# First weights over a second DMA queue, gamma scaled on POOL, a column for variance plus epsilon

## The chip, the cores and the metric

The kernel runs on one core of a Trainium2 chip. The core has five engines that work from queues of their own: PE (matrix multiply), DVE (vector), ACT (activation functions), POOL (general purpose) and SP (here it only starts transfers). The metric is the device time of one execution in microseconds, taken as the median over runs. In the profile, "PEld" is the loading of weights into PE, which overlaps its matmuls, and "SPq", "ACTq", "POOLq" stand for instructions that an engine's sequencer handles, such as the start of a DMA transfer.

## The reference

One layer of a decoder over 512 tokens of width 1024 in float32. Cut to what matters:

```python
proj = h @ w_in                                   # q, k, v, pool input, gates
y_attn = moba_attention(q, k, v, rel_bias) @ w_branch_attn
y_pool = multiscale_pool(p, w_pool_group, pool_scale) @ w_branch_pool
mixed  = sigmoid(g0) * y_attn + sigmoid(g1) * y_pool
h = layer_norm(ALPHA * h + mixed @ w_out, ln1_g, ln1_b)
a, u = split(h @ w_ffn_in)
f = (gelu(causal_dwconv(a, conv_w, conv_b)) * u) @ w_ffn_out
h = layer_norm(ALPHA * h + f, ln2_g, ln2_b)

def layer_norm(x, g, b):
    mu = x.mean(-1); var = ((x - mu) ** 2).mean(-1)
    return (x - mu) * rsqrt(var + 1e-5) * g + b
```

## The kernel before

Every matrix product is made of three passes: each float32 operand is split into a rounded high part (`hi`, type fp32r) and a remainder (`lo`), and `mm3` (lines 144 to 148) adds hi x hi, hi x lo and lo x hi into one PSUM bank. The splitting is done by `split` (line 63): ACT copies the source into `hi` (line 67) and DVE subtracts `hi` from the source (line 68). A caller may pass another function for the copy; for the first tile of x that is DVE's `tensor_copy`.

Weights come in chunks of 128 x 1024 elements. `fetch` (line 92) takes the next chunk of a fixed list, starts its transfer from SP (line 108) into one of three raw buffers (tag `wraw`), and splits it into one of five `whi` and `wlo` buffers. `weights(i)` calls `fetch` until it is three chunks ahead of the matmuls. The very first chunk is fetched in two halves of 512 columns, and between the two the second half of the first x tile is loaded (the `early` argument). `load_x` (line 171) loads and splits the eight tiles of the transposed x. Before all of this PE makes eight matmuls on zeros (`WARM`, line 168), and ACT runs an activation on one column (line 164), which loads its function table.

The stages in order: the value projection (line 240); the other input projections interleaved with the attention heads; the two branch projections and their merge (`mt`, line 437, on POOL, then split into `mx_hi` and `mx_lo`); the output projection (`wo`); the first normalization; the feed-forward input (`fi`) with convolution and gelu; the feed-forward output as seven products of a block scheme (`PRODUCTS`, line 40); the second normalization and the stores. The program text gives each engine's order only in part: a scheduler places instructions of independent work on each engine by a time model, so work written later can stand ahead of work written earlier. On one engine everything then runs in its queue's order, so an instruction that waits holds back what stands behind it.

In the seven products the left operands alternate between two buffers, `sd[0]` and `sd[1]`, and the splits of the next product's operand (`sd_hi`, `sd_lo`) are placed as soon as the columns that they overwrite have been read. The weights of some products are formed in the buffer `tw`: after `tw` has been split, a transfer started from POOL adds the next weights to it (line 134).

The two normalizations share their code. `ln_rows` (line 447) loads one gamma row and one beta row, spread over all 128 partitions, by a transfer started from POOL, and multiplies the gamma by -0.5 on ACT (line 450). In the second normalization it is called behind the sixth product, and SP then copies the beta rows to the output (line 711), onto which finished rows are added later. `moments` (line 470) aggregates mean and variance on DVE, takes the root of variance plus epsilon on ACT (`rstd` column 0) and adds epsilon to the variance on DVE (line 474). `centre` (line 484) computes (x - mu) times the scaled gamma, `invert` (line 477) takes the reciprocal of the root and improves it by one step with variance plus epsilon, and `rescale` (line 488) multiplies by the result and adds beta. The last 128 rows go through `finish` (line 508), where DVE's order is the written one.

Of the kernel before, what the change touches and what calls it, by code (L numbers as in the profile page):

```python
# [8 lines left out]
F32 = mybir.dt.float32  # L9
F32R = mybir.dt.float32r  # L10
AF = mybir.ActivationFunctionType
ALU = mybir.AluOpType
PSUM = bass.MemoryType.PSUM

P = 128
# [3 lines left out]
NT = S // P  # L19
# [8 lines left out]
EPS = 1e-5  # L28
# [3 lines left out]
LEAD = 3  # L32
RING = 5
TMP = 4
WARM = 8
NKEEP = 12
NLATE = 4
KH = NF // 2
# [5 lines left out]
def layer_kernel(ctx: ExitStack, tc: tile.TileContext, xT, x, w_v, w_c, rel_bias, invcnt, w_group,  # L44
                 pscale, w_br, w_out, lnr, w_fi, convp, w_fo, out):
    nc = tc.nc
    const = ctx.enter_context(tc.tile_pool(name="const", bufs=1))
# [8 lines left out]
    def bank(name):  # L56
        return ps.tile([P, S], F32, tag="ps", name=name)
# [5 lines left out]
    def split(hi, lo, src, copy=None):  # L63
        if copy:
            copy(hi, src)
        else:
            nc.scalar.activation(hi, src, AF.Copy)  # L67
        nc.vector.tensor_tensor(lo, src, hi.bitcast(F32), op=ALU.subtract)  # L68
# [9 lines left out]
    chunks = [w_v[c] for c in range(4)]  # L78
# [13 lines left out]
    def fetch(pool=None, early=None):  # L92
        i = state["next"]
        state["next"] = i + 1
        if isinstance(chunks[i], tuple):
            ready[i] = fetch_fo(i, *chunks[i])
            return
        raw = wp.tile([P, D], F32, tag="wraw", name=f"wraw{i}", bufs=3)
        if pool is None:
            hi = wp.tile([P, D], F32R, tag="whi", name=f"whi{i}", bufs=RING)  # L100
            lo = wp.tile([P, D], F32R, tag="wlo", name=f"wlo{i}", bufs=RING)
        else:
            hi = pool.tile([P, D], F32R, name=f"whi{i}")
            lo = pool.tile([P, D], F32R, name=f"wlo{i}")
        parts = 2 if early else 1
        for c in range(parts):
            sl = slice(c * (D // parts), (c + 1) * (D // parts))
            nc.sync.dma_start(raw[:, sl], chunks[i][:, sl])
            split(hi[:, sl], lo[:, sl], raw[:, sl])
            if c == 0 and early:  # L110
                early()
        ready[i] = (hi, lo)
# [7 lines left out]
    def fetch_fo(i, name, c):  # L120
        sl = piece(c)
        n = sl.stop - sl.start
        step = {"T3": "=B11", "B11": "+B12", "T1": "+B22", "T2": "+B21", "T4": None}
        if name in step:
            raw = tw[:, sl]
        else:
            raw = wp.tile([P, D], F32, tag="wraw", name=f"wraw{i}", bufs=3)[:, :n]
            nc.sync.dma_start(raw, half(name, sl))
        hi = wp.tile([P, D], F32R, tag="whi", name=f"whi{i}", bufs=RING)[:, :n]
        lo = wp.tile([P, D], F32R, tag="wlo", name=f"wlo{i}", bufs=RING)[:, :n]  # L130
        split(hi, lo, raw)
        then = step.get(name)
        if then and then[0] == "+":
            nc.gpsimd.dma_start(raw, half(then[1:], sl), accum_op=ALU.add)  # L134
        elif then:
            nc.sync.dma_start(raw, half(then[1:], sl))
        return hi, lo

    def weights(i):
        while state["next"] <= min(i + LEAD, state["limit"]):  # L140
            fetch()
        return ready[i]
# [6 lines left out]

    def split3(v, a):  # L150
        return tuple(t.rearrange("p (a c) -> p a c", a=a) for t in v)

    xT_hi = act.tile([P, KT, S], F32R, tag="actT_hi", name="xT_hi")
    xT_lo = act.tile([P, KT, S], F32R, tag="actT_lo", name="xT_lo")
# [12 lines left out]
    wb_ = bank("warm_ps")  # L167
    for i in range(WARM):
        nc.tensor.matmul(wb_, warm[:, :P], warm, start=True, stop=True)
# [5 lines left out]
    for kt in range(KT):  # L175
        xr = aw.tile([P, S], F32, tag="tmp", name=f"xr{kt}", bufs=TMP)
        if kt == 0:
            load_x(kt, xr, slice(0, 256), nc.vector.tensor_copy)
            fetch(early=lambda: load_x(kt, xr, slice(256, 512), nc.vector.tensor_copy))
        else:  # L180
            load_x(kt, xr)
            if kt % 2 == 0:
                fetch()
# [44 lines left out]
    for kt in range(KT):  # L228
        wh, wl = split3(weights(kt // 2), 2)
        wh, wl = wh[:, kt % 2, :], wl[:, kt % 2, :]  # L230
        xs_ = [(xT_hi[:, kt, j * P:(j + 1) * P], xT_lo[:, kt, j * P:(j + 1) * P]) for j in range(NT)]
        last = kt == KT - 1
        if last:
            for j in range(NT):
                mm3(bs[j], xs_[j], (wh, wl), False, True)
                nc.scalar.activation(vv[:, j, :], bs[j], AF.Copy)
        else:
            for n, (a, b) in enumerate(((0, 0), (1, 0), (0, 1))):
                for j in range(NT):
                    nc.tensor.matmul(bs[j], xs_[j][a], (wh, wl)[b], start=kt == 0 and n == 0, stop=False)  # L240
# [55 lines left out]
    def in_tile(n):  # L296
        kind, j = order[n]
        wh, wl = split3(weights(C0 + n), KT)
        b = bank(f"{kind}{j}")
        for kt in range(KT):  # L300
            mm3(b, (wh[:, kt, :], wl[:, kt, :]), (xT_hi[:, kt, :], xT_lo[:, kt, :]), kt == 0, kt == KT - 1)
        if kind == "q":
            q_done(j, b)
        elif kind == "k":
            k_done(j, b)
        elif kind == "p":
            pool_in(j, b)
        elif len(gslot) < NKEEP:
            gslot[j] = gates[:, len(gslot), :]
            nc.vector.tensor_copy(gslot[j], b)  # L310
        else:
            gslot[j] = late[:, len(gslot) - NKEEP, :]
            nc.scalar.activation(gslot[j], b, AF.Sigmoid)
# [106 lines left out]
    for f in range(KT):  # L420
# [7 lines left out]
        for br in (1, 0):  # L428
            b = bank(f"br{f}_{br}")
            for k in range(4):  # L430
                src = (zT_hi[:, k, :], zT_lo[:, k, :]) if br else (oT_hi[:, k, :], oT_lo[:, k, :])
                mm3(b, (wh[:, 4 * br + k, :], wl[:, 4 * br + k, :]), src, k == 0, k == 3)
            t = bp.tile([P, S], F32, tag="m", name=f"m{f}_{br}", bufs=4)
# [13 lines left out]
    def ln_rows(r):  # L447
        t = hw.tile([P, 2, D], F32, tag="lnb", name=f"lnb{r}")
        nc.gpsimd.dma_start(t, bass.AP(tensor=lnr.tensor, offset=lnr.offset + r * D, ap=[[0, P], [D, 2], [1, D]]))
        nc.scalar.activation(t[:, 0, :], t[:, 0, :], AF.Copy, scale=-0.5)  # L450
        return t

    lnb = ln_rows(0)
    ypool = ctx.enter_context(tc.tile_pool(name="ypool", bufs=1, reuse_waits="tile"))
    ytiles = [ypool.tile([P, S], F32, name=f"y{j}") for j in range(2)]
# [3 lines left out]
    hT_lo = hTp.tile([P, KT, S], F32R, name="hT_lo")  # L459
    st = const.tile([P, NT, 4, 6], F32, name="st")  # L460
    mv = const.tile([P, NT, 2], F32, name="mv")
    rstd = const.tile([P, NT, 2], F32, name="rstd")

    def add_residual(i, c0, c1, b):
        sl = xs[:, i, c0:c1]
# [4 lines left out]
    def moments(i):  # L470
        mu, var = mv[:, i, 0:1], mv[:, i, 1:2]
        nc.vector.bn_aggr(mv[:, i, :], st[:, i].rearrange("p a b -> p (a b)"))
        nc.scalar.activation(rstd[:, i, 0:1], var, AF.Sqrt, bias=eps_t)
        nc.vector.tensor_scalar(var, var, EPS, None, op0=ALU.add)
        return mu, var

    def invert(i, var, pin=lambda ins: ins):
        r, t = rstd[:, i, 0:1], rstd[:, i, 1:2]
# [14 lines left out]
    def scale_out(i):  # L493
        mu, var = moments(i)
        centre(i, slice(0, D), mu)
        r = invert(i, var)
        nc.scalar.activation(xs[:, i, :], xs[:, i, :], AF.Copy, scale=r)
        nc.gpsimd.dma_start(out[i * P:(i + 1) * P, :], xs[:, i, :], accum_op=ALU.add)

    def share_out(i):  # L500
        mu, var = moments(i)
        centre(i, slice(0, D), mu)
        r = invert(i, var)
        nc.scalar.activation(xs[:, i, right], xs[:, i, right], AF.Copy, scale=r)
        rescale(i, left, r)
        nc.gpsimd.tensor_tensor(xs[:, i, right], xs[:, i, right], lnb[:, 1, right], op=ALU.add)

    def finish(i):
        pin = tc.keep_in_program_order
        mu, var = moments(i)  # L510
        pin(centre(i, right, mu))
        r = invert(i, var, pin)
        nc.scalar.activation(xs[:, i, rest], xs[:, i, rest], AF.Copy, scale=r)
        pin(centre(i, left, mu))
        nc.gpsimd.tensor_tensor(xs[:, i, rest], xs[:, i, rest], lnb[:, 1, rest], op=ALU.add)
        pin(rescale(i, left, r))
        pin(rescale(i, most, r))
# [106 lines left out]
    for j in range(RING, 2 * NF):  # L624
        hb[j] = bank(f"fi{j}")
        fi_mm(j, hb[j], slice(0, S))
        if j % 2:
# [3 lines left out]
            if f % 2 == 0 and f >= 6 and f < 6 + 2 * NC:  # L631
                c = f // 2 - 3
# [74 lines left out]
    gather(3, S, D, bank_a[1], 1, False, False)  # L707
    product(5, bank_d, False)
    lnb = ln_rows(2)
    for i in range(2):  # L710
        nc.sync.dma_start(out[i * P:(i + 1) * P, :], lnb[:, 1, :])
# [89 lines left out]
```

## Time and profile before

| | us |
|---|---|
| Time, median of 3 runs | 662.54 (662.19 to 663.27) |
| Profiled execution, its own time | 663.32 |
| Its span in the profile | 661.6 |
| PE busy | 649.4 |
| DVE busy | 384.4 |
| ACT busy | 285.9 |
| POOL busy | 89.3 |
| DMA: read and written | 80.01 MB and 3.17 MB |

The times in the profile count from the start of the span. A line of the timeline has the start, the duration, the engine, the source line, the operation, output and inputs with their shapes, and in brackets the idle time before it and what ended it. The mean clock granted to PE over the execution was 0.997 of full speed. What is called a wait is put down to the semaphore that came last.

### The profile page before, as it was taken

The page shows a single profiled execution, that of the slowest core. Times are in us where ns is not written, and L with a number is a line of the kernel's source. Part 1 is how long each engine was busy: PE and PEld are TensorE (multiplying, and loading weights), DVE is VectorE, ACT ScalarE, POOL GpSimd, SP SyncE. Part 2 cuts the span into 40 slices and gives each one's busy share as a digit, 9 for nine tenths or more (in the row PEclk, how much of TensorE's full clock was granted, in tenths as well). Part 3 has the DMA queues.
Part 4 walks back from the last instruction along what each step waited for, and adds up shares of the span by engine and source line. Part 5 has one row for each costly group of instructions (what it writes and reads, how often), then busy time and mean ns, then how long its engine had stood idle before and what let it go on. Part 6 is the DMA issues. An engine that isn't in the chain of part 4 may idle for free.

```text
span 661.6 us, 8020 instructions
## 1 busy us (share of the span) xinstructions
PE 649.4 (98%) x3083; PEld 538.8 (81%) x3083; DVE 384.4 (58%) x559; ACT 285.9 (43%) x395; POOL 89.3 (14%) x137
## 2 busy tenths in 40 slices
PE   8999999999999999999999999999999999999994
PEld 6888787877888888889988888888888888888874
DVE  5556665554532675398456344443534548788596
ACT  5646556675422332232443333333323236555452
POOL 0705261211000124002100000000000001124002
PEclk9999999999999999999999999999999999999998
DMA  8643222222322227208942222233233334989905
GB/s 285 215 150 118 80 79 80 73 74 79 96 95 96 93 98 291 91 1 292 251 157 97 96 95 96 95 100 101 99 97 97 104 100 97 211 188 203 261 1 127
DMA packets 24918, 83.70 MB, mean 127 GB/s; under 512 B 3240, under 2 KB 3496, under 8 KB 24624
## 3 DMA queue, kind: packets, MB, share of 16 engines
q1 hardware_dynamic: 19312, 63.77, 29.1%
q0 software_dynamic: 5280, 18.90, 13.2%
q8 instruction: 24, 0.39, 0.2%
q10 hardware_dynamic: 288, 0.52, 0.2%
q14 instruction: 14, 0.11, 0.1%
HBM read 80.01 MB, written 3.17 MB: 126 GB/s over the span
## 4 chain that ended last, share of the span: by engine, by line
PE 77%; issue 10%; DMA 4%; POOL 4%; DVE 3%; ACT 1%; POOLq 0%; DVEq 0%; SPq 0%; ACTq 0%
PE fi L147 11%; PE fi L146 11%; PE fi L148 11%; PE g L146 4%; PE g L147 4%; PE g L148 4%; PE v L240 3%; PE wo L146 2%; PE br L147 2%; PE br L146 2%; PE wo L147 2%; PE wo L148 2%; PE br L148 2%; POOL tw L134 2%; PE ob L372 1%
## 5 line engine op out<-in xcount | busy, mean ns | idle before, releaser
L68 DVE TENSOR_TENSOR wlo<-wraw,whi 128x1024 fp32r<-128x1024 f32 (+1 forms) x105 | 134.3, 1284 | 119.8 <-ACT whi L67 117.9
L67 ACT ACTIVATE whi<-wraw 128x1024 fp32r<-128x1024 f32 (+1 forms) x105 | 109.0, 1041 | 187.4 <-PE fi L147 84.0
L147 PE MATMUL fi<-hT_lo,whi 128*128 128x512 f32 (+1 forms) x392 | 143.8, 367 | 0.0
L148 PE MATMUL fi<-hT_hi,wlo 128*128 128x512 f32 (+1 forms) x392 | 143.8, 367 | 0.0
L146 PE MATMUL fi<-hT_hi,whi 128*128 128x512 f32 (+1 forms) x392 | 143.5, 368 | 0.0
L148 PEld LDWEIGHTS fi<-hT_hi,wlo 128*128 128x128 f32 x392 | 73.9, 189 | 12.3
L147 PEld LDWEIGHTS fi<-hT_lo,whi 128*128 128x128 f32 x392 | 73.9, 189 | 12.0
L146 PEld LDWEIGHTS fi<-hT_hi,whi 128*128 128x128 f32 x392 | 73.6, 189 | 12.2
L134 POOL DMA_DIRECT2D tw<-in_w_fo x18 | 15.8, 906 | 269.9 <-DVE wlo L68 269.9
L146 PE MATMUL g<-xT_hi,whi 128*128 128x512 f32 x128 | 50.3, 393 | 0.0
L148 PE MATMUL g<-xT_hi,wlo 128*128 128x512 f32 x128 | 49.9, 390 | 0.0
L147 PE MATMUL g<-xT_lo,whi 128*128 128x512 f32 x128 | 49.8, 389 | 0.0
L67 ACT ACTIVATE whi<-tw 128x1024 fp32r<-128x1024 f32 (+1 forms) x30 | 29.4, 983 | 25.4 <-PE fi L147 11.3
L578 DVE TENSOR_TENSOR fT<-y,fi 128x512 f32<-128x512 f32 x22 | 15.1, 687 | 40.0 <-PE fi L148 39.2
L68 DVE TENSOR_TENSOR wlo<-tw,whi 128x1024 fp32r<-128x1024 f32 (+1 forms) x30 | 33.3, 1126 | 8.6 <-ACT whi L67 8.4
L577 ACT ACTIVATE y<-y 128x512 f32<-128x512 f32 x22 | 13.9, 632 | 43.0 <-DVE y L576 43.0
L148 PEld LDWEIGHTS g<-xT_hi,wlo 128*128 128x128 f32 x128 | 24.0, 188 | 5.1
L146 PEld LDWEIGHTS g<-xT_hi,whi 128*128 128x128 f32 x128 | 24.0, 188 | 5.0 <-issue 0.2
L147 PEld LDWEIGHTS g<-xT_lo,whi 128*128 128x128 f32 x128 | 24.0, 188 | 4.8
L345 POOL TENSOR_SCALAR pp<-pp,rs 128x128 f32<-128x128 f32 (+3 forms) x32 | 21.8, 698 | 37.7 <-PE g L148 18.4
L146 PE MATMUL wo<-whi,mx_hi 128*128 128x512 f32 x64 | 25.0, 390 | 0.0
L148 PE MATMUL wo<-whi,mx_lo 128*128 128x512 f32 x64 | 24.9, 389 | 0.0
(202 smaller groups left out, 1169.7 us busy)
## 6 DMA issues: line engine op xcount, KB each, us to landing
wraw<-in_w_fi SPq DMA_DIRECT2D x44, 512.0 KB, 3.3
wraw<-in_w_c SPq DMA_DIRECT2D x28, 512.0 KB, 3.4
tw<-in_w_fo POOLq DMA_DIRECT2D x20, 512.0 KB, 7.6
tw<-in_w_fo SPq DMA_DIRECT2D x10, 512.0 KB, 3.9
wraw<-in_w_fo SPq DMA_DIRECT2D x10, 512.0 KB, 5.2
wraw<-in_w_br SPq DMA_DIRECT2D x8, 512.0 KB, 3.3
wraw<-in_w_out SPq DMA_DIRECT2D x8, 512.0 KB, 3.4
strip<-F_d POOLq DMA_DIRECT2D x8, 256.0 KB, 3.5
```

What stands on the lines that cost most here:

```text
L67: nc.scalar.activation(hi, src, AF.Copy)
L68: nc.vector.tensor_tensor(lo, src, hi.bitcast(F32), op=ALU.subtract)
L134: nc.gpsimd.dma_start(raw, half(then[1:], sl), accum_op=ALU.add)
L146: nc.tensor.matmul(out_, wh, ah, start=start, stop=False, **kw)
L147: nc.tensor.matmul(out_, wh, al, start=False, stop=False, **kw)
L148: nc.tensor.matmul(out_, wl, ah, start=False, stop=stop, **kw)
L240: nc.tensor.matmul(bs[j], xs_[j][a], (wh, wl)[b], start=kt == 0 and n == 0, stop=False)
L345: nc.gpsimd.tensor_scalar(pp[:, offs[i]:offs[i] + n], pp[:, offs[i]:offs[i] + n], rs[:, i:i + 1], 1.0, op0=ALU.mult, op1=ALU.mult)
L372: nc.tensor.matmul(b[e * DH:(e + 1) * DH, kb * P:], vv[:, kb, h * DH:(h + 1) * DH], PTs[h][:, toff[kb]:toff[kb] + n], start=kb == 0, stop= ...
L577: nc.scalar.activation(y, y, AF.Gelu)
L578: nc.vector.tensor_tensor(fT[:, j, :], y, u, op=ALU.mult)
```

## The change

The first chunk's two half transfers are started by ACT instead of SP. Its first half is copied to `hi` by two engines: DVE takes columns 0 to 191 and ACT columns 192 to 511; its second half is split as before. One warm-up matmul less is made. Gamma is multiplied by -0.5 on POOL instead of ACT, in both normalizations. Variance plus epsilon is written to a column of its own in `rstd`, which is widened from two columns to six, instead of over the variance.

On the engines this means: SP's queue loses its second and fourth instruction. ACT's queue begins with the first half's transfer, ahead of the table load; the second half's transfer stands behind the one-column activation. DVE's queue has the copy of 192 columns between the remainder of x's first half tile and the copy of its second half. On POOL the first gamma product stands behind the last `mt`, ahead of the transfers into `tw`; the second stands behind the transfer of its rows and two transfers into `tw`, and ahead of the last two transfers into `tw`. On DVE the addition of epsilon stands ahead of the centring in every row instead of behind it; in the last row it did so before. All other queues keep their order.

```diff
-WARM = 8
+WARM = 7
@@ fetch
-            nc.sync.dma_start(raw[:, sl], chunks[i][:, sl])
-            split(hi[:, sl], lo[:, sl], raw[:, sl])
+            (nc.scalar if early else nc.sync).dma_start(raw[:, sl], chunks[i][:, sl])
+            split(hi[:, sl], lo[:, sl], raw[:, sl], fast if early and c == 0 else None)
@@ new, before the x tiles
+    def fast(hi, src):
+        for copy, c in ((nc.vector.tensor_copy, slice(0, 192)), (first_copy, slice(192, 512))):
+            copy(hi[:, c], src[:, c])
+
+    def first_copy(hi, src):
+        nc.scalar.activation(hi, src, AF.Copy)
@@ ln_rows
-        nc.scalar.activation(t[:, 0, :], t[:, 0, :], AF.Copy, scale=-0.5)
+        nc.gpsimd.tensor_scalar(t[:, 0, :], t[:, 0, :], -0.5, None, op0=ALU.mult)
@@ normalization
-    rstd = const.tile([P, NT, 2], F32, name="rstd")
+    rstd = const.tile([P, NT, 6], F32, name="rstd")
@@ moments
-        nc.vector.tensor_scalar(var, var, EPS, None, op0=ALU.add)
-        return mu, var
+        nc.vector.tensor_scalar(rstd[:, i, 2:3], var, EPS, None, op0=ALU.add)
+        return mu, rstd[:, i, 2:3]
```

## The prediction

> **What bounds the kernel now.** I read the page's busy lines first, then everything PE waited for, then the timeline at the places where the edits act: the opening, the gamma of each normalization, the last rows.
>
> ```profile
> span 661.6 us, 8020 instructions
> PE 649.4 (98%) x3083; PEld 538.8 (81%) x3083; DVE 384.4 (58%) x559; ACT 285.9 (43%) x395; POOL 89.3 (14%) x137
> ```
>
> ```profile
> PE warm_ps L169 <- DVE warm L166: 1.3, 1, 1.3
> PE v L240 <- ACT whi L67: 0.7, 1, 0.7
> PE fod L147 <- DVE wlo L68: 0.7, 1, 0.7
> PE zb L146 <- ACT difh L67: 0.5, 2, 0.3
> ```
>
> PE is busy for 649.4 of 661.6 us, and the second block (total us, times, longest) is the whole list of its waits: 3.2 us. The rest of its idle time lies behind its last matmul. So an edit gains only where PE waits or after PE has ended: at the first weights ("v"), at one wait near the end ("fod") and in the last rows. "zb" hangs on POOL and ACT work of the attention part, which no edit touches. Everything else is judged by whether it makes PE wait.
>
> **The opening** (start us, duration, engine, line):
>
> ```profile
> 0.81 1.28 ACT L164 ACT_TABLE_LOAD   x1 [0.81 <-PEq L793]
> 1.25 0.42 SPq L108 DMA_DIRECT2D wraw<-in_w_v  x1
> 2.19 0.43 SPq L108 DMA_DIRECT2D wraw<-in_w_v  x1
> 4.23 0.63 PE L169 MATMUL warm_ps<-warm 128*128 128x512 bf16 x1
> 4.91 0.63 ACT L67 ACTIVATE whi<-wraw 128x512 fp32r<-128x512 f32 x1 [2.60 <-DMA wraw<-in_w_v]
> 5.59 1.22 PE L240 MATMUL v<-whi,xT_hi 128*128 128x512 f32 x2 [0.73 <-ACT whi L67]
> 6.70 0.63 ACT L67 ACTIVATE whi<-wraw 128x512 fp32r<-128x512 f32 x1 [1.16 <-DMA wraw<-in_w_v]
> 7.35 1.28 ACT L67 ACTIVATE xT_hi<-xr 128x512 fp32r<-128x512 f32 x2
> 9.18 0.62 PE L240 MATMUL v<-whi,xT_lo 128*128 128x512 f32 x2
> 10.10 1.08 PE L240 MATMUL v<-whi,xT_hi 128*128 128x512 f32 x4
> ```
>
> ```profile
> 265.01 1.04 ACT L450 ACTIVATE lnb<-lnb 128x1024 f32<-128x1024 f32 x1
> ```
>
> The chain is: issue at 1.25, data at 4.91 (3.66 later), ACT's copy of 0.63, first real matmul at 5.59. After the change ACT issues this transfer ahead of its table load, near 0.82: 0.43 earlier. The copy shrinks: ACT takes 0.63 for 512 columns and 1.04 for 1024, so 0.8 ns a column, and 0.63 - 192 x 0.0008 = 0.48 for its 320; DVE's 192 columns run beside it. That is 0.15. The first matmul comes to 5.59 - 0.43 - 0.15 = 5.0.
>
> It brings less than it moves. The eight matmuls from 5.59 to 9.18 start 0.45 apart, the four from 9.18 to 10.10 0.23 apart: PE begins at half speed. If the speed still changes at 9.18, 0.58 us of head start is 1.3 slow matmuls, worth 1.3 x 0.23 = 0.3; if the change moves along with the start, it is 0.58. I take **0.4**. The bounds: PE cannot start before its seventh warm-up matmul is through (the eighth starts at 4.23), so 1.36 at most; at the other end the transfer, now side by side with SP's, lands up to 0.94 later than I count (another 128 x 512 x 4 bytes, 0.26 MB, as much as its own, at the 278 GB/s of a full stretch quoted with the rivals): a first matmul at 5.95, a loss of 0.36. I stay near 0.4 because the row of this same transfer is the nearest there is.
>
> A rule speaks against more: the Trainium skill ("DMA: Bandwidth & Descriptors", Issuing engines are not separate DMA queues) says that transfers started by several engines run on the same 16 engines and that only the starting engine's issue time is saved. By it the 0.43 stays and the lower bound of the start, 4.23, is out of reach.
>
> What lies behind these edits: ACT's table load, dummy and second issue slide by 0.4, under the 2.60 that ACT idles before 4.91. The second half is issued near 2.8 instead of 2.19, its copy starts near 7.3 instead of 6.70, and the xT_hi behind it near 7.95 instead of 7.35, done 0.64 later at 8.6; PE comes to it about 9.6 (10.10 less the gain). Cover 1 us, and past that every delay is PE's. DVE's small copy pushes the cast of xr's second half by under 0.4, which PE needs four slow matmuls after its start: 1.8 of cover. SP loses two issues (0.42 + 0.43), so its later ones come up earlier: 0, since PE waits for none. WARM 7 removes one warm-up matmul that would end before the weights are there: 0.
>
> **Gamma on POOL.** The first time (the group's columns: busy, mean ns, idle before):
>
> ```profile
> 262.31 2.14 POOL L437 TENSOR_TENSOR mt<-m,m 128x512 f32<-128x512 f32 x1 [7.12 <-DVE m L434]
> 283.44 1.40 DVE L485 SCALAR_TENSOR_TENSOR xs<-xs,mv,lnb 128x512 f32<-128x512 f32 x2
> 308.48 0.94 POOL L634 DMA_DIRECT2D tw<-in_w_fo  x1 [44.03 <-DVE hT_lo L68]
> ```
>
> ```profile
> L345 POOL TENSOR_SCALAR pp<-pp,rs 128x512 f32<-128x512 f32 x8 | 6.5, 816 | 0.0
> ```
>
> POOL's price for 1024 columns is at most 2 x 0.816 = 1.6 us. POOL is through with mt at 264.45, gamma is ready near 266.1, its first reader starts at 283.44, and the next work in POOL's queue at 308.48. Cost 0; with that cover gone, 1.6 less the 1.04 that ACT loses. The second time is another matter:
>
> ```profile
> 610.38 1.76 POOL L134 DMA_DIRECT2D tw<-in_w_fo  x2 [1.73 <-DVE wlo L68]
> 611.36 0.39 PE L148 MATMUL foa<-whi,sd_lo 128*128 128x512 f32 x1
> 613.88 1.73 SPq L711 DMA_DIRECT2D out<-lnb  x2
> 613.95 1.06 ACT L450 ACTIVATE lnb<-lnb 128x1024 f32<-128x1024 f32 x1 [4.25 <-DMA lnb<-in_lnr]
> 614.91 1.04 ACT L67 ACTIVATE sd_hi<-fT 128x1024 fp32r<-128x1024 f32 x1
> 632.43 0.39 PE L146 MATMUL foe<-whi,sd_hi 128*128 128x512 f32 x1
> 633.48 0.50 PE L147 MATMUL fod<-wlo,sd_hi 128*128 128x512 f32 x1 [0.66 <-DVE wlo L68]
> ```
>
> ```profile
> 617.13 1.23 DVE wlo L68
> 618.37 8.18 DMA wraw<-in_w_fo
> 632.30 1.14 DVE wlo L68
> ```
>
> The second fence is the chain that ended last. ACT stands 4.25 us for gamma's rows with sd_hi in its queue behind them, and this is what makes PE wait later: sd_hi starts at 614.91, DVE splits the next weights at 617.13, only then is a raw buffer free and SP issues the next transfer (618.37); it lands 8.18 later, and the last split of DVE's run behind it ends at 633.44 with PE standing. Without gamma, sd_hi waits only for the last matmul that reads the columns which it overwrites (611.36): it starts near 611.8, 3.1 earlier. The transfer then goes out when SP is through with its own two issues: 613.88 + 1.73 = 615.6, 2.75 earlier than 618.37. PE lost 633.48 - 632.43 - 0.23 = 0.8, which a move of 2.75 covers. Gain **0.8**; bounds 0 and 0.9 (a slow first matmul, 0.50 where 0.39 is usual). Late next is the split of the last half chunk, in the same run of DVE and moved with it.
>
> In exchange POOL stands: the two accumulating transfers of 610.38 queue behind gamma and go out near 613.9 + 1.6 = 615.5, 5 us later. They feed the last two pieces of tw:
>
> ```profile
> tw<-in_w_fo POOLq DMA_DIRECT2D x1, 256.0 KB, 14.8
> ```
>
> ```profile
> L67 ACT ACTIVATE whi<-tw x18: 633/1046/1063, 582.6 to 640.0; 128x1024 fp32r<-128x1024 f32 x15, 128x512 fp32r<-128x512 f32 x3
> ```
>
> Even the slowest landing of this stretch, 14.8 us, gives 631.2 for the second issue (616.4 + 14.8), and the last piece is read at 640.0. Cost 0; with 9 us more it would hit PE directly.
>
> **Variance plus epsilon.** In the tail nothing covers anything:
>
> ```profile
> 653.58 0.26 DVE L472 BATCH_NORM_AGGREGATE mv<-st 128x2 f32<-128x24 f32 x1
> 653.87 0.30 ACT L473 ACTIVATE rstd<-mv,eps_t 128x1 f32<-128x1 f32 x1 [1.77 <-DVE mv L472]
> 654.20 0.15 DVE L474 TENSOR_SCALAR mv<-mv 128x1 f32<-128x1 f32 x1 [0.36 <-ACT rstd L473]
> 656.23 1.59 DVE L489 SCALAR_TENSOR_TENSOR xs<-xs,rstd,lnb 128x512 f32<-128x512 f32 x2
> ```
>
> The addition wrote over the variance that ACT's root reads, so DVE stood 0.36 until the root was done. With its own column it follows the aggregate at once, and the centring behind it is longer than the root (0.30). DVE's queue moves up by the 0.36, up to the rescaling and the last stores. Gain **0.35**; bounds 0.2 and 0.4. The other seven rows, and the order of additions and centrings in them, lie under PE: 0. The wider rstd: 0.
>
> **Sum.** 0.4 + 0.8 + 0.35 = 1.55 us off the profiled execution, which took 663.32 us (1.72 around the span); it lies 0.78 above the median of the runs. From the median: 662.54 - 1.55 = **661.0 us**.
>
> **The rivals.** They rest on these stretches (length, PE, PEld, DVE, ACT, POOL, clock, share of DMA, GB/s):
>
> ```profile
> 618.00:622.00 4.00, 4.00 (x19) 3.31 (x18) 4.00 (x5) 1.75 (x2) 0.00 (x0) 1.00 1.05 278
> 622.00:627.00 5.00, 5.00 (x24) 4.13 (x23) 1.54 (x3) 0.34 (x1) 0.00 (x0) 1.00 1.03 363
> 627.00:632.00 5.00, 5.00 (x24) 4.14 (x23) 4.25 (x7) 4.82 (x6) 0.00 (x0) 1.00 0.05 19
> ```
>
> (1) The fod wait stays. The DMA engines are full until 627, and the two moved transfers (0.79 MB) now travel with the weights: at 278 to 363 GB/s that is 2.2 to 2.8 us, just the 2.75 gained. Against it: the moved transfers leave room before 615. Then 0.75 off: 661.8.
> (2) PE is at full speed sooner. In the trace the speed changes 3.59 after PE's last pause (5.59 to 9.18); that pause was 0.73 and would now be about 0.57. If the shorter pause no longer counts, the matmuls from 5.0 run 0.23 apart, the first twelve end at 7.8 and PE waits for xT_hi until 8.6 where it was at 10.10: 1.5 instead of 0.4, so 2.65 off: 659.9. This is what the Trainium skill ("TensorE: Matmul & The Clock Gate", Part 1) would allow: the full clock comes after a busy window of 3.4 us whose edges do not follow the kernel.
> (3) The opening loses its 0.36 and the rest holds: 0.8 off, 661.7. For it speaks that all transfers share full engines; against it, that the first ones go out while the engines are still empty.
> (4) Slower: the wraw transfer that goes out at 615.6 lands as late as the slowest beside it, 14.8 later at 630.4 instead of 626.55. PE then stands 3.9 longer than before, less 0.4 and 0.35: 665.7. It decides past a landing of about 13 us. Against it: the engines run empty at 627.
>
> **How the numbers follow.** A measurement of this kernel tells 0.2%, 1.3 us, from no change. Forecast 0.53; (1) 0.21; (2) 0.13; (3) 0.07; (4) 0.06. The forecast's own range, from its bounds, is 660.3 to 661.6, and some seven tenths of it lie below 661.2: 0.37, which with (2) and the edges of (1) and (3), 0.05, makes faster 0.55. Same is the rest of the forecast, of (1) and of (3): 0.39. Slower is (4): 0.06. The range leaves out (4) and the far end of (2), and reaches past (1) by the 0.4 that the opening may give less: 659.5 to 662.2.
>
> **What would show it.** Right: first v matmul near 5.0; no PE wait at fod; sd_hi near 611.8, ACT without a wait for lnb; DVE's 0.36 before the addition gone, the span near 660.1. Wrong: the first wraw landing later than 4.5; PE at half speed beyond 9.2; a new wait of PE or ACT for wraw at 624 to 634 or for tw near 640.

## The result, and the profile after

The changed kernel takes 664.49 us (median of 17 runs, 663.35 to 665.98), the kernel before 662.19 (17 runs, 661.19 to 664.5): a ratio of 1.003 with an interval of 1.0021 to 1.004. It is slower by 0.3%, where 661.0 and faster was forecast, and it lies outside the range. The profiled execution took 664.89 us, its span was 663.1.

The busy lines of the changed kernel, and everything PE waited for (total us, times, longest):

```profile
span 663.1 us, 8016 instructions
PE 651.5 (98%) x3082; PEld 537.1 (81%) x3082; DVE 385.3 (58%) x560; ACT 284.1 (43%) x393; POOL 94.6 (14%) x139
```

```profile
PE warm_ps L176 <- DVE warm L173: 1.3, 1, 1.3
PE v L247 <- DVE whi L155: 0.4, 1, 0.4
```

This is odd at first sight. PE waits less than before: 1.7 us in all against 3.2, the fod wait is gone as forecast, and no new wait has come. Yet PE is busy for 2.1 us more (651.5 against 649.4) with one matmul less. So the loss is in the matmuls themselves. A view in which instructions are grouped by their tile shows where (count, then duration in ns as min/median/max, then first and last start in us). The kernel before:

```profile
L146 PE MATMUL g<-xT_hi,whi x128: 389/389/499, 99.0 to 214.1; 128*128 128x512 f32 x128
L147 PE MATMUL fob<-wlo,sd_hi x22: 389/389/389, 576.4 to 590.7; 128*128 128x512 f32 x22
L146 PE MATMUL fi<-hT_hi,whi x392: 277/389/396, 303.6 to 545.6; 128*128 128x512 f32 x156, 128*128 128x256 f32 x40
```

The kernel after:

```profile
L146 PE MATMUL g<-xT_hi,whi x128: 393/394/502, 97.3 to 215.0; 128*128 128x512 f32 x128
L147 PE MATMUL fob<-wlo,sd_hi x22: 394/394/394, 577.9 to 592.3; 128*128 128x512 f32 x22
L146 PE MATMUL fi<-hT_hi,whi x392: 277/389/396, 304.9 to 546.9; 128*128 128x512 f32 x156, 128*128 128x256 f32 x40
```

The gate matmuls (`g`) start 1.7 us earlier than before (97.3 against 99.0) and end 0.9 later (215.0 against 214.1): the same stage, with the same instructions, takes 117.7 instead of 115.1. The durations of single matmuls have grown from 389 to 394 ns. `fob` shows the same in small (the line shown is the longest of its three passes; the other two take 392 and 388), and `fi`, with the same weights buffers and the same kind of instruction, does not: its first and last start have both moved by 1.3. The stretch from 100 to 210 us, before and then after (PE, PEld, DVE, ACT, POOL, clock, share of DMA, GB/s), speaks against the throttle and the DMA as its cause:

```profile
100.00:210.00 110.00, 110.00 (x530) 88.72 (x530) 52.55 (x96) 59.59 (x97) 10.75 (x17) 1.00 0.26 84
```

```profile
100.00:210.00 110.00, 110.00 (x520) 86.82 (x519) 50.77 (x93) 58.66 (x96) 10.71 (x17) 1.00 0.23 82
```

In both the clock is granted in full and PE is never idle, but it gets through 520 matmuls instead of 530.

The places at which the edits were meant to act went about as forecast. The opening after (start, duration, engine, line):

```profile
0.79 0.41 ACTq L108 DMA_DIRECT2D wraw<-in_w_v  x1
3.86 0.47 ACT L158 ACTIVATE whi<-wraw 128x320 fp32r<-128x320 f32 x1 [1.13 <-DMA wraw<-in_w_v]
4.65 0.70 PE L247 MATMUL v<-whi,xT_hi 128*128 128x512 f32 x2 [0.40 <-DVE whi L155]
5.19 0.62 PE L247 MATMUL v<-whi,xT_lo 128*128 128x512 f32 x2
7.48 1.07 PE L247 MATMUL v<-whi,xT_hi 128*128 128x512 f32 x4
```

The first real matmul starts at 4.65 (forecast 5.0, before 5.59) and the matmuls from 5.19 on start 0.23 apart. The thirteenth, which stood at 10.10, starts at 7.48. The second gamma and what hangs on it, after:

```profile
613.18 1.06 ACT L67 ACTIVATE sd_hi<-fT 128x1024 fp32r<-128x1024 f32 x1 [1.89 <-PE foa L147]
615.06 3.07 POOL L457 TENSOR_SCALAR lnb<-lnb 128x1024 f32<-128x1024 f32 x1 [4.83 <-DMA lnb<-in_lnr]
615.42 3.19 DVE L68 TENSOR_TENSOR wlo<-wraw,whi 128x1024 fp32r<-128x1024 f32 x2
617.51 4.98 SPq L128 DMA_DIRECT2D wraw<-in_w_fo  x3
618.09 1.82 POOL L134 DMA_DIRECT2D tw<-in_w_fo  x2
```

ACT no longer stands for gamma's rows: sd_hi waits only for the matmul that reads what it overwrites. And the tail, after:

```profile
654.14 0.26 DVE L479 BATCH_NORM_AGGREGATE mv<-st 128x2 f32<-128x24 f32 x1
654.43 0.15 DVE L481 TENSOR_SCALAR rstd<-mv 128x1 f32<-128x1 f32 x1
656.47 1.59 DVE L496 SCALAR_TENSOR_TENSOR xs<-xs,rstd,lnb 128x512 f32<-128x512 f32 x2
```

The addition follows the aggregate without the 0.36, and the last rescaling comes 2.33 us behind the aggregate instead of 2.65.

The thirteenth matmul and this last rescaling (it stood at 656.23 before) bound a stretch that leaves out the opening and the last stores. It is 656.23 - 10.10 = 646.13 us before and 656.47 - 7.48 = 648.99 after: 2.86 longer, although two waits in it (fod, and the 0.36) are gone. It is used below as "the stretch".

### The profile page after: what moved, and what is told of

Read it like the earlier page. It is cut to its first block, busy times and chain, and to the rows that moved or that the text cites. A ratio compares the mean times of both kernels' runs of the same rounds, so it can differ in the third digit from the quotient of the medians.

```text
span 663.1 us, 8016 instructions
## 1 busy us (share of the span) xinstructions
PE 651.5 (98%) x3082; PEld 537.1 (81%) x3082; DVE 385.3 (58%) x560; ACT 284.1 (43%) x393; POOL 94.6 (14%) x139
## 4 chain that ended last, share of the span: by engine, by line
PE 98%; DVE 1%; DMA 0%; issue 0%; DVEq 0%
PE fi L147 12%; PE fi L146 12%; PE fi L148 12%; PE g L146 5%; PE g L148 5%; PE g L147 5%; PE v L247 3%; PE wo L146 2%; PE wo L148 2%; PE wo L147 2%; PE br L147 2%; PE br L148 2%; PE br L146 2%; PE fod L147 2%; PE foa L147 2%; PE foa L146 2%
## 5 line engine op out<-in xcount | busy, mean ns | idle before, releaser
L444 POOL TENSOR_TENSOR mt<-m,m 128x512 f32<-128x512 f32 x8 | 11.2, 1394 | 97.6 <-DVE m L441 80.9
```

The costliest lines, as they stand in the source:

```text
L444: nc.gpsimd.tensor_tensor(mt, m[1], m[0], op=ALU.add)
```

## The experiments

**The theory.** The one edit that reaches PE's matmuls in the first third of the kernel without waiting for anything is the wider `rstd`. It adds 4 x 4 columns of 4 bytes, 64 bytes a partition, to the `const` pool, and the pools behind it on the same side of the memory move by 64 bytes: the weights (`whi`, `wlo`), `hT` and others. `xT`, `sd[0]` and the few buffers laid out from the other end stay where they are. In the built programs `whi0` lies at byte 31424 before and at 31488 after, `xT_hi` at 196544 in both. Counted modulo 256 that is 192 and 192 before, 0 and 192 after. In the slow stages one operand of the matmul has moved and the other has not (`g`: weights and `xT`; `fob`: weights and `sd[0]`); in `fi` both have moved (weights and `hT`). In `g` the weights are the stationary operand (the one that is loaded into PE) and `xT` the moving one (the one that is streamed through it); in `fob` `sd[0]` is stationary and the weights move. So the theory is that the spacing of PE's matmuls depends on how the addresses of its two operands lie to each other. The rivals are that the new column, or the other edits, cost the time, and that the address itself counts, not the difference.

**Only the wider rstd.** The kernel before with that one line:

```diff
-    rstd = const.tile([P, NT, 2], F32, name="rstd")
+    rstd = const.tile([P, NT, 6], F32, name="rstd")
```

> The kernel before with rstd widened from two to six columns and nothing else; the four new columns are used by nobody. The widening moves every buffer that is allocated behind rstd on the left side of SBUF by 64 bytes (the weight buffers from byte 31424 to 31488 of a partition), while those on the right side (xT, mx, sd[0]) stay. Address theory: matmuls whose two operands come one from the left and one from the right start further apart, 0.233 instead of 0.227 us in q, k, p and g, up to 215 us; normal spacing in br and fi, where both operands are on the left. From the stages of the changed kernel that is 4.0 us before br, 0.4 in wo and 0.4 in the products: about 4.8 us slower than before, 666 to 667. Start theory (the slower spacing comes from PE running at full speed from its first real matmul on): spacing 0.227 throughout, time as before within 1 us.

Measured: 666.6 us, ratio 1.0066 (1.0047 to 1.0085). The four added columns are read and written by nothing. By tile, this kernel:

```profile
L146 PE MATMUL g<-xT_hi,whi x128: 393/394/502, 100.1 to 217.8; 128*128 128x512 f32 x128
L147 PE MATMUL fob<-wlo,sd_hi x22: 394/394/394, 580.7 to 595.1; 128*128 128x512 f32 x22
L146 PE MATMUL fi<-hT_hi,whi x392: 277/389/396, 307.7 to 549.7; 128*128 128x512 f32 x156, 128*128 128x256 f32 x40
```

The same 394 and 394, the same 117.7 us for the gates, and `fi` untouched. The cause of the loss lies in this line, without any of the other edits.

**The other end moved instead.** The kernel before, with the pad at the other end of the memory larger by 64 bytes, so that `xT` and `sd[0]` move and the weights stay:

```diff
-    edge.tile([P, 8], F32, name="edge_t")
+    edge.tile([P, 24], F32, name="edge_t")
```

> The kernel before with the unused tile at the right end of SBUF 24 columns wide instead of 8: now the right side moves by 64 bytes and the left stays. Address theory, if what counts is that the two operands differ: as the first run, 666 to 667, with 0.233 in q to g. If what counts is the left side's own address: time as before. Start theory: as before.

Measured: 665.96 us, 1.0063 (1.0044 to 1.0082). The gates of this kernel:

```profile
L146 PE MATMUL g<-xT_hi,whi x128: 393/394/496, 100.2 to 217.9; 128*128 128x512 f32 x128
```

They take 117.7 us again. `rstd` is as before here and all weights lie at their old bytes; the difference of the operands alone is that of the first run. So not the address of the weights counts, but how it stands to that of the other operand.

**128 bytes apart, made in two ways.** The changed kernel with `rstd` of ten columns (weights 128 bytes behind their first place), and the changed kernel with the larger pad (weights 64 one way, `xT` 64 the other):

```diff
-    rstd = const.tile([P, NT, 6], F32, name="rstd")
+    rstd = const.tile([P, NT, 10], F32, name="rstd")
```

> The changed kernel with rstd ten columns wide instead of six, so that the left side moves by 128 bytes and not by 64. Address theory: spacing 0.227 in all stages, and the gains of the opening (2.6 us at the thirteenth matmul), of the zb waits (0.5) and of the tail (0.3) are left: 658.5 to 660.0, faster than before by 0.3 to 0.5%. Start theory, or any theory in which another edit slows PE: 0.233 in q to g as in the changed kernel, 664 to 665.

```diff
-    edge.tile([P, 8], F32, name="edge_t")
+    edge.tile([P, 24], F32, name="edge_t")
```

> The changed kernel, rstd six columns wide, with the unused tile at the right end 24 columns wide: both sides have moved by 64 bytes. Address theory, operands that differ: 658.5 to 660.0 as with ten columns, spacing 0.227. Theory of the left side's own address, or start theory: 664 to 665.

Measured: 665.65 us, 1.0056 (1.0039 to 1.0073), and 665.75, 1.0059 (1.0038 to 1.008). Both misses: I had taken the grain for 128 bytes, and 128 is as bad as 64. But the two, which have the same difference and share no address, give the same time and the same new pattern. The first of them by tile:

```profile
L146 PE MATMUL g<-xT_hi,whi x128: 390/393/496, 97.9 to 215.4; 128*128 128x512 f32 x128
L147 PE MATMUL fob<-wlo,sd_hi x22: 390/393/404, 579.0 to 593.6; 128*128 128x512 f32 x22
```

**256 bytes.** The changed kernel and the kernel before, both with `rstd` of 18 columns, 256 bytes a partition more than two:

```diff
-    rstd = const.tile([P, NT, 6], F32, name="rstd")
+    rstd = const.tile([P, NT, 18], F32, name="rstd")
```

> The changed kernel with rstd 18 columns wide, so that the left side moves by 256 bytes against the kernel before. In the kernel before all operand buffers of PE, left and right, lie at 192 above a multiple of 256; 64 and 128 bytes of difference between the sides were slow. Theory of 256: only the difference modulo 256 counts, spacing 0.227 everywhere, and what the edits bring is left: PE 2.6 us ahead at the thirteenth matmul, no zb wait, a tail shorter by 0.3: 658.5 to 660.0. Theory that any move of one side against the other is slow, or that an edit of the change itself slows PE: 664 to 666, spacing 0.229 to 0.233.

```diff
-    rstd = const.tile([P, NT, 2], F32, name="rstd")
+    rstd = const.tile([P, NT, 18], F32, name="rstd")
```

> The kernel before with rstd 18 columns wide and nothing else (the new columns are used by nobody). Theory of 256: spacing 0.227, time as before within 0.2%. Any-move theory: 666, as with six columns.

Measured: the changed kernel takes 660.14 us, 0.9961 (0.9946 to 0.9977), the kernel before so padded 662.29, 0.9996 (0.9985 to 1.0006). The gates of the second one:

```profile
L146 PE MATMUL g<-xT_hi,whi x128: 389/389/499, 97.3 to 212.3; 128*128 128x512 f32 x128
```

With a whole 256 bytes the loss is gone, and the other edits show what they are worth: 0.39%, 2.6 us. More bytes cost nothing by themselves.

**The widening undone.** The whole change, but variance plus epsilon goes to a buffer of four columns that is no longer needed by then, and `rstd` keeps two:

```diff
-    rstd = const.tile([P, NT, 6], F32, name="rstd")
+    rstd = const.tile([P, NT, 2], F32, name="rstd")
...
-        nc.vector.tensor_scalar(rstd[:, i, 2:3], var, EPS, None, op0=ALU.add)
-        return mu, rstd[:, i, 2:3]
+        nc.vector.tensor_scalar(psc[:, i:i + 1], var, EPS, None, op0=ALU.add)
+        return mu, psc[:, i:i + 1]
```

> All of the change, but rstd stays at two columns: variance plus epsilon goes to psc, four columns that are dead by then, so no buffer behind rstd moves. Theory of 256 (PE's matmuls start 0.227 us apart only where the addresses of its two operands agree modulo 256 bytes): as the run with 18 columns, 0.9961 of before, 660.0, the g matmuls 389 ns, 90 matmuls in the stretch of 180 to 200. Rival (the new column itself or its place in DVE's queue costs, not the addresses): slow, 664 to 665, g at 393.

Measured: 659.82 us, 0.9961 (0.9947 to 0.9975): the same as with 18 columns. This kernel's span, what PE waited for, and the gates:

```profile
span 657.9 us, 8016 instructions
```

```profile
PE warm_ps L176 <- DVE warm L173: 1.2, 1, 1.2
PE zb L146 <- ACT difh L67: 0.5, 2, 0.3
PE v L247 <- DVE whi L155: 0.5, 1, 0.5
```

```profile
L146 PE MATMUL g<-xT_hi,whi x128: 389/389/499, 96.7 to 211.8; 128*128 128x512 f32 x128
```

Every edit of the change is in this kernel, and it is faster than before by 2.6 us. The gates are back at 389 ns and 115.1 us. The stretch is 644.81 here and in the run with 18 columns (652.64 - 7.83 and 653.12 - 8.31): 1.32 shorter than before, 4.18 shorter than in the changed kernel. That 4.18 is what the widening cost it in these profiles.

**Other differences.** The changed kernel with 14 columns (192 bytes behind), and the kernel before with four (32 bytes):

```diff
-    rstd = const.tile([P, NT, 6], F32, name="rstd")
+    rstd = const.tile([P, NT, 14], F32, name="rstd")
```

> rstd of 14 columns: everything behind it 192 bytes further than before. Theory of 256 and a cost that depends on the distance to the next multiple of 256 (64, from the other side): as the change itself, 1.003 of before, 664.5, or as 128 bytes off, up to 666. If any multiple of 64 off costs the same kind of loss: 664 to 666. Rival (only 64 and 128 are bad): 660.2, g at 389.

```diff
-    rstd = const.tile([P, NT, 2], F32, name="rstd")
+    rstd = const.tile([P, NT, 4], F32, name="rstd")
```

> Before with rstd of four columns: 32 bytes further. If the grain is 32 bytes or finer, slow: 664 to 667, g at 391 to 393. If only whole steps of 64 count: as before, 662.5, g at 389. What a difference of 32 does was not seen before; slow is taken as the likelier.

Measured: 664.53 us, 1.0032 (1.0019 to 1.0046), and 667.65, 1.0069 (1.0046 to 1.0092). The last one by tile:

```profile
L146 PE MATMUL g<-xT_hi,whi x128: 392/396/498, 98.1 to 215.7; 128*128 128x512 f32 x128
L147 PE MATMUL fob<-wlo,sd_hi x22: 393/395/397, 579.5 to 594.2; 128*128 128x512 f32 x22
L146 PE MATMUL fi<-hT_hi,whi x392: 279/389/396, 306.1 to 548.1; 128*128 128x512 f32 x156, 128*128 128x256 f32 x40
```

`fob` runs without a gap in all these kernels: 22 matmuls of each of three passes, so that the first and the last of one pass are 63 starts apart. That makes 14.3 / 63 = 0.227 us a matmul before, 14.4 / 63 = 0.229 at 64 bytes, 14.6 / 63 = 0.232 at 128 and 14.7 / 63 = 0.233 at 32.

The direction counts as well. The address of the stationary operand less that of the moving one, modulo 256, is 64 in `g` and 192 in `fob` in the changed kernel, and in the kernel with 14 columns it is the other way round:

```profile
L146 PE MATMUL g<-xT_hi,whi x128: 388/388/505, 98.4 to 214.5; 128*128 128x512 f32 x128
L147 PE MATMUL fob<-wlo,sd_hi x22: 393/396/398, 578.2 to 592.9; 128*128 128x512 f32 x22
```

`g` takes 117.7 us at 64 and 116.1 at 192, against 115.1 at 0; `fob` 14.7 at 64 and 14.4 at 192, against 14.3. In both stages 64 costs more than 192.

Nor does every matmul get slower. Among the last ones are 66 of 256 columns (`fo_cut`), with `sd[0]` stationary and the weights moving as in `fob`. Before and after:

```profile
L146 PE MATMUL fo_cut<-whi,sd_hi x22: 277/283/283, 637.7 to 652.1; 128*128 128x256 f32 x22
L146 PE MATMUL fo_cut<-whi,sd_hi x22: 276/276/279, 638.7 to 652.7; 128*128 128x256 f32 x22
```

They got shorter, 276 ns instead of 283, and from the first to the last it is 14.0 us instead of 14.4.

All in one table, by the shift of one side of the memory against the other; a kernel is compared with the same kernel at difference 0:

| shift of one side against the other, bytes | kernels | against the same kernel at 0 |
|---|---|---|
| 32 | before, four columns | 1.0069 |
| 64 | before, six columns; before, larger pad; the change itself | 1.0066; 1.0063; 1.003 / 0.9961 = 1.007 |
| 128 | change, ten columns; change, larger pad | 1.0056 / 0.9961 = 1.010; 1.010 |
| 192 | change, 14 columns | 1.007 |
| 256 | before, 18 columns; change, 18 columns | 0.9996; the base |

**Gamma on POOL alone.** The kernel before with this one edit:

```diff
-        nc.scalar.activation(t[:, 0, :], t[:, 0, :], AF.Copy, scale=-0.5)
+        nc.gpsimd.tensor_scalar(t[:, 0, :], t[:, 0, :], -0.5, None, op0=ALU.mult)
```

> The kernel before with gamma scaled on POOL and nothing else; no buffer moves. My prediction's step: ACT's sd_hi starts near 612, the transfer behind it goes out near 615.6, the fod wait of PE (0.8) goes: 0.8 us faster. Rival, from the changed kernel's trace, where that transfer landed at 627.6 although it went out earlier and POOL's multiplication took 3.1 us: the landing is set by full DMA engines, the wait stays, time as before within 0.4 us.

Measured: 661.21 us, 0.9982 (0.9971 to 0.9992), 1.2 us less. This kernel's wait, its queues and its chain at the place:

```profile
PE fod L147 <- DVE wlo L68: 0.5, 1, 0.5
```

```profile
610.26 1.06 ACT L67 ACTIVATE sd_hi<-fT 128x1024 fp32r<-128x1024 f32 x1 [1.86 <-PE foa L147]
612.13 3.08 POOL L450 TENSOR_SCALAR lnb<-lnb 128x1024 f32<-128x1024 f32 x1 [4.78 <-DMA lnb<-in_lnr]
612.50 3.19 DVE L68 TENSOR_TENSOR wlo<-wraw,whi 128x1024 fp32r<-128x1024 f32 x2
```

```profile
614.58 10.55 DMA wraw<-in_w_fo
```

The transfer went out at 614.58 instead of 618.37, in a program that was 1.25 ahead at the thirteenth matmul (8.85 against 10.10): 2.5 of it is the edit's, near the 2.75 forecast. But it took 10.55 instead of 8.18, so most of the lead was lost in the DMA engines, which are full all the while (a share of 1.02 to 1.06 from 614.6 to 625.1), and PE still waited 0.5. That is the mechanism of rival (1), of a size in between. The stretch is 0.16 shorter than before (654.82 - 8.85 = 645.97), less than the 1.2 of the times. In five of the six kernels with all the edits the wait is gone, in the one with 14 columns it is 0.2. Over all profiles it lies between 0 and 1.2 without this edit (six, mean 0.7) and between 0 and 0.5 with it (seven, mean 0.1).

**The opening alone.** The kernel before with the edits to the warm-up, the two transfers and the first copy:

```diff
-WARM = 8
+WARM = 7
...
-            nc.sync.dma_start(raw[:, sl], chunks[i][:, sl])
-            split(hi[:, sl], lo[:, sl], raw[:, sl])
+            (nc.scalar if early else nc.sync).dma_start(raw[:, sl], chunks[i][:, sl])
+            split(hi[:, sl], lo[:, sl], raw[:, sl], fast if early and c == 0 else None)
```

> The kernel before with the opening's edits alone (first weights over ACT's queue, split by DVE and ACT, seven warm-up matmuls); no buffer moves. From the changed kernel's trace: thirteenth matmul near 7.5 instead of 10.1, all of it kept to the end by PE, less what waits at zb and fod give back or take: 2 to 3 us faster, 659.0 to 660.2. If the start at full speed makes later matmuls slower: no gain, spacing over 0.227. If full speed comes by chance of the start's phase: single times between 659 and 662.

Measured: 661.85 us, 0.9987 (0.9975 to 1.0), 0.9 us less (0 to 1.7 by the interval), where I had come to expect 2 to 3 from the two first profiles. They had misled me: the opening differs from one execution to the next. The kernel before with the unused 18 columns, whose opening is the old one in every instruction:

```profile
1.24 0.42 SPq L108 DMA_DIRECT2D wraw<-in_w_v  x1
3.95 0.63 ACT L67 ACTIVATE whi<-wraw 128x512 fp32r<-128x512 f32 x1 [1.65 <-DMA wraw<-in_w_v]
4.63 1.22 PE L240 MATMUL v<-whi,xT_hi 128*128 128x512 f32 x2
6.51 0.64 PE L240 MATMUL v<-whi,xT_hi 128*128 128x512 f32 x2
8.37 1.07 PE L240 MATMUL v<-whi,xT_hi 128*128 128x512 f32 x4
```

The same transfer landed 1 us earlier than in the profile before (3.95 against 4.91), PE changed its speed at 6.51 instead of 9.18, and the thirteenth matmul starts at 8.37 instead of 10.10. Over all profiles the thirteenth matmul starts between 7.92 and 10.34 with the old opening (six profiles, mean 9.3) and between 7.48 and 8.31 with the new one (seven, mean 8.0). The new opening brings about 1.3 there, and it does away with the late cases. Alone it may return part of that at the fod wait, which is 1.2 in this kernel instead of 0.7; as that wait varies from profile to profile, this is not shown.

## Why the prediction was wrong

**The step that failed is "The wider rstd: 0."** I priced the columns as an instruction's operand, and they cost nothing as such: 18 of them in the kernel before make 0.9996. What I left out is that an allocation moves all that lies behind it. It cost 4.4 us in the kernel before (666.6 and 1.0066) and 4.18 us in the stretch of the changed kernel. No row of the profile before could have priced it, since the two operands of every projection and product agree there modulo 256 (in the built program only the small attention matmuls `ob` and the transposes do not), but the diff shows a size that changes in the first pool. The chances allowed nothing for it; slower had 0.06, for another mechanism.

**The opening: 0.4 forecast, 0.9 to 1.3 found.** The times of that edit alone give 0.9, the mean start of the thirteenth matmul 1.3. The first matmul near 5.0 was right (4.65 to 5.17 in the profiles with this opening). The term was mis-sized because I read the speed change at 9.18 as fixed, to the start of the program or to PE's first matmul. The same instructions changed speed at 6.51 in another execution. The Trainium skill ("TensorE: Matmul & The Clock Gate", Part 1) says that the window behind the change runs freely and that the count of slow matmuls varies from run to run; the profiles agree, with a change at 9.18 and at 6.51 under one and the same opening. Rival (2), full speed from the start, is what the changed kernel's profile shows, though not what all its executions can be said to do. Its reason, that a shorter pause no longer counts, is not borne out. The kernel with gamma alone and the one with the opening alone begin so:

```profile
6.00 0.73 PE L240 MATMUL v<-whi,xT_hi 128*128 128x512 f32 x2 [1.15 <-ACT whi L67]
5.17 0.70 PE L247 MATMUL v<-whi,xT_hi 128*128 128x512 f32 x2 [0.73 <-DVE whi L155]
```

Both are near full speed from the first pair on, behind pauses of 1.15 and 0.73, where the kernel before stood 0.73 and began at half speed. So no rule by the length of the pause comes out of these profiles, and whether the new opening makes the fast start likelier they do not settle.

**Gamma on POOL: 0.8 forecast, 1.2 by the times (0.5 to 1.9 by the interval), 0.6 by the mean fod waits.** The mechanism was right: ACT's wait is gone, the transfer goes out some 2.5 earlier, and in the changed kernel's profile PE doesn't wait at fod. Two sizes were off. POOL took 2.77 to 3.55 us for gamma, not 1.6 at most; the tw transfers behind it went out at 618.09 instead of 615.5, and the cover held, since PE has no wait for their splits. And DVE's two subtractions beside it took 3.19 instead of 2.35. In the kernel with gamma alone the 8.18 of the transfer became 10.55, the loss that rival (1) named.

**Variance plus epsilon: 0.35 forecast, 0.32 found** (2.65 to 2.33 between aggregate and rescaling).

**The sum without the failed step.** 1.55 was forecast, and 2.6 is what the same edits bring when no buffer moves (659.82 and 660.14). In the stretch it is 1.32 against 0.8 + 0.35 = 1.15, and the rest is the opening. Rivals (3) and (4) did not come: the first transfers landed earlier, not later, and no transfer near the end made PE stand. The range within the forecast, 660.3 to 661.6, does not follow from the bounds that stand with the three gains: they add up to 2.66 off at one end and 0.16 more at the other, 659.9 to 662.7. The result lies above both.

Why PE's matmuls start further apart when the addresses of their operands differ modulo 256 isn't settled, nor why those of 256 columns did not. That the loading of weights, which overlaps the matmul before it, is disturbed by that matmul's own reading would fit; no run takes the two apart.

## What to carry to other kernels

When a change makes an allocation larger or smaller, list where the buffers behind it come to lie, and keep the two operands of PE's matmuls of 512 columns at the same address modulo 256, if need be by a pad or by the use of a dead buffer. For other widths measure it: the 256-column matmuls here were a little faster with their operands apart. If PE is busy for longer without waiting for longer, compare the durations of the same tile in both profiles before looking for a wait. The kernel without the widening, at 659.82 us, is faster than both (0.9961 of before), and one pair of profiles is not enough to price an opening whose start varies by more than 2 us.

## What was not expected of the hardware

PE's matmuls of 512 columns in this kernel start 0.227 us apart when the addresses of stationary and moving operand agree modulo 256, and 0.229 to 0.233 apart in `fob` when one side is shifted by 32, 64, 128 or 192 bytes, at a granted clock of 1.00 and with PE never idle. Which operand lies ahead matters: `fob` takes 14.7 us at 64 and 14.4 at 192. By all the runs this is 0.6 to 1.0% of the kernel, though `fi`, the longest stage, was never touched. No shift below 32 bytes was run. The Trainium skill ("TensorE: Matmul & The Clock Gate", Back-to-back issue gap) gives the gap by the number of columns and the state of the clock; here it depends on the addresses as well.

POOL holds DVE up. While POOL multiplied 1024 columns in the kernel with gamma alone, DVE's pair of subtractions took 3.19 us, where it took 2.35 in the kernel before, without POOL beside it:

```profile
617.13 2.35 DVE L68 TENSOR_TENSOR wlo<-wraw,whi 128x1024 fp32r<-128x1024 f32 x2
```

Whether DVE holds POOL up as much is not shown: POOL's multiplication took 2.77 to 3.55 us, more than the 1.6 estimated, but always with DVE's subtractions beside it. The Trainium skill ("SBUF — State Buffer", Who interferes with whom) says that a DVE instruction with two inputs in SBUF contends with a GpSimd (POOL) instruction that reads SBUF; the trace agrees, with those 0.84 us.
